# The first four m-tiles of a hybrid block on G*(x-s), corrected on their products, with the adaLN rounds in runs

## The chip, the cores and the metric

One core of one Trainium2 chip runs the whole program. The metric is the device time of one execution in microseconds. Before the change three runs took 2303.6 to 2304.38 us, median 2304.2 us.

## The reference, cut to what matters

Two post-LN layers, 512 latent tokens (l) and 256 context tokens (c), width 2048. Each layer modulates its normalised input by adaLN, projects it into the inputs of three mixers (latent attention, RG-LRU, retention), gates their outputs and projects back. What the change touches is the very beginning, for layer 0:

```python
mod = silu(cond) @ w_ada + b_ada          # shift, scale, gate; one set for l, one for c
h   = layer_norm(x) * (1 + scale) + shift # = G*(x-mu)*rstd + B
u   = h @ w_in                            # its columns: lru_x (512), lru_g, ret_..., mla_...
```

With s the value that is subtracted from x of a token first, layer_norm(x) is (x-s)*rstd - rmean, where rmean = (mu-s)*rstd. So h @ w is rstd*((G*(x-s)) @ w) - rmean*(G @ w) + B @ w.

## The kernel before, in words

Tensors lie transposed: 16 k-tiles of 128 features, each 128x512 (l) or 128x256 (c). Every fp32 product is done in three: the weight (`wh`, `wl`) and the token tile (`xh`, `xl`) are split in a high and a low part, and TensorE adds wh*xh, wh*xl and wl*xh into one PSUM tile. ScalarE copies the high parts, VectorE subtracts for the low ones. The order on each engine is the order in which the program calls it; nothing reorders. Background tasks (`spawn`) are generators; `step()`, called after every step of matmuls, resumes the first two of its list, or the first alone where a task is marked so. All loads are issued by SP, in one queue, by `fetch` (L168); every engine call is recorded at L158, every matmul at L204, transposes at L208.

The opening (L1515 to L1618) is written out by hand:

- SP loads all 16 k-tiles of x (256 KB) and c (128 KB), then the first 16 adaLN tiles, then three `wing` tiles (the weights of lru_x, 512 KB each, eight in all). Of the adaLN weights `wada` the opening reads 16 blocks of eight 128x512 tiles.
- The statistics: s is the mean of the first k-tile, VectorE subtracts it from x, ScalarE squares, TensorE adds both up with a 32-column matrix of ones; `fold2`, `finish` and `spread` make rstd and rmean, broadcast over the partitions.
- `Ada.steps` (L403) computes two blocks of adaLN: 16 `wada` tiles, 64 matmuls of 256 columns, in which four positions of 32 columns of the array each take one matmul of a set. Each set of four ends with a `yield`. Then ScalarE copies the result out, TensorE transposes it and VectorE reduces it.
- `first_norm` normalises two k-tiles in place (VectorE multiplies, POOL subtracts); `first` makes G and B for two k-tiles (`gb_block`), then h and its split: a VectorE multiply-add per tile (`x_high`), a high copy on ScalarE, a low part on VectorE. Into `res` go the tiles that are kept for later.
- `group(xps, j2, ...)` (L1582) multiplies k-tiles 2*j2 and 2*j2+1 into all four lru_x m-tiles: eight steps, of one k-tile and one m-tile each, six matmuls a step. The sums of all 16 k-tiles stay in PSUM: two `pa` tiles (two m-tiles of l each) and two `pb` tiles (of c). After each step `pause()` does the next set of the adaLN block that group j2+2 needs. So groups 0 to 5 have sets of adaLN between their steps and groups 6 and 7 have none.
- After group 7 `lru_pad` copies the four products into padded tiles, by turns on ScalarE and VectorE. It frees the `pa` tiles, of which there are two; the next projection (lru_g, in layer 0's loop from L1624) takes the first. The LRU tasks (convolution, gates, recurrence) are spawned then, behind `softplus_neg`.

`W` is the stream of projection weights: three buffers of 512 KB (`ws`), five high and four low parts; `W.get` hands out one k-tile and prepares the next four or five. Pools: `L` 48 tiles of 128x512, `C` 50 of 128x256, `aw` 3 of 128x512, `big` 2 of 128x1552, `pa` 2, `pb` 4.

Of the kernel before, what the change touches and what calls it, by code (L numbers as in the profile page):

```python
# [17 lines left out]
P = 128  # L18
# [18 lines left out]
AHEAD = 12  # L37
KEEP = {"l": 10, "c": 0}
# [47 lines left out]
def hybrid_kernel(ctx: ExitStack, tc: tile.TileContext, a, out_l):  # L86
# [140 lines left out]
    class Weights:  # L227
# [3 lines left out]
        def __init__(self, srcs, packed):  # L231
            self.srcs, self.packed, self.n, self.st, self.hl = srcs, packed, 0, {}, {}
# [35 lines left out]
        def prepare(self, i):  # L268
            for k in range(5):
                self.high(i + k)  # L270
                if k < 4:
                    self.low(i + k)

        def get(self):
            i = self.n
            self.n += 1
            self.prepare(i)
            self.load((i + 5) // 2)
            self.load((i + 7) // 2)
            return self.hl.pop(i)[:2]  # L280
# [109 lines left out]
    class Ada:  # L390
        def __init__(self, order):
            self.todo = [(cbs, n, q) for cbs in order for n in range(len(cbs)) for q in range(8)]
            self.w, self.n, self.nl = {}, 0, 0

        def load(self, i, slot):
            while self.nl < min(i, len(self.todo)):
                cbs, n, q = self.todo[self.nl]
# [5 lines left out]
        def steps(self, slot, ahead):  # L403

            cbs = self.todo[self.n][0]
            ps = PB()
            for n in range(len(cbs)):
                for q in range(0, 8, 2):
                    self.load(self.n + ahead, slot)
# [83 lines left out]

    def gb_block(l, j, n):

        for i in range(2):
# [5 lines left out]
            if l == 0:  # L502
                V.tensor_copy(B, sh)
            else:
                tt(B, G, pv(l - 1, "ln_b", j, n), op=OP.mult)
                tt(B, B, sh, op=OP.add)
                tt(G, G, pv(l - 1, "ln_g", j, n), op=OP.mult)
# [52 lines left out]
    def fold2(src, T):  # L560

        n = T // P
        ps = PB()
        for t in range(n):
            transpose(ps[:, t * P:(t + 1) * P], src[:, t * P:(t + 1) * P])
        v = ps[:, :T].rearrange("p (t g k r) -> p k t g r", g=2, k=2, r=32)
        o = SM(n, "fold"), SM(n, "fold")
        for k in range(2):
            V.tensor_reduce(o[k], v[:, k], axis=AX.XY, op=OP.add)
        return o  # L570

# [7 lines left out]
    class Stat:  # L579
        def __init__(self, T, parts, later=None):  # L580
            self.T = T
            self.s, self.sd, self.qd, self.sq = (v[:, 0:T] for v in parts)
            self.r, self.m = (v[:, 0:T] for v in later) if later else (self.s, self.sq)
# [23 lines left out]
        def finish(self, eps, rows=1):  # L607
            n = self.T // P
            if rows > 1:
                s, q = fold2(self.sd, self.T)  # L610
            else:
                yield self.sd, self.qd
                s = fold(self.sd, self.T)
                q = fold(self.qd, self.T)
            mu, v, t = SM(n, "st_mu"), SM(n, "st_v"), SM(n, "st_t")
            ts(mu, s, 1.0 / (D * rows), None, op0=OP.mult)
            tt(t, mu, mu, op=OP.mult)
            ts(v, q, 1.0 / (D * rows), eps, op0=OP.mult, op1=OP.add)
# [137 lines left out]
    def lru_pad(pss, b, eng):  # L756
# [3 lines left out]
        for s in "lc":  # L760
            o = b[:, PAD[s] + 2:PAD[s] + 2 + NT[s]]
            if eng == "a":
                copyA(o, pss[s])
            else:
                V.tensor_copy(o, pss[s])
# [750 lines left out]
    AD = Ada([(8 + j, j) for j in range(8)])  # L1516

    z0 = {"l": [], "c": []}
    stats, acc = {}, {}
    for j in range(NK):  # L1520
        for s, src in (("l", a["xT"]), ("c", a["cT"])):
            z = ST(s)
            fetch(z, src[j])
            z0[s].append(z)
    AD.load(16, LT)
    W.load(0)
    W.load(1)
    W.load(2)
    for s in "lc":
        b = BIG()  # L1530
        stats[s] = Stat(NT[s], [LT() for _ in range(4)], (b[:, 0:512], b[:, 512:1024]))
        ps = PB()
        mm(ps[:, :NT[s]], ones, z0[s][0], start=True, stop=True)
        copyA(stats[s].s, ps[:, :NT[s]])
    for s in "lc":
        acc[s] = PB()
    for j in range(NK + 1):
        for i, s in enumerate("lc"):
            T, st = NT[s], stats[s]
            if j < NK:  # L1540
                z = z0[s][j]
                tt(z, z, st.s, op=OP.subtract)
                act((st.sq, st.qd)[j % 2], z, AF.Square)
                g = 64 * ((j + i) % 2)
                mm(acc[s][g:g + 32, :T], one32, z, start=(j < 2), stop=(j >= NK - 2), tile_position=(0, g),
                   skip_group_check=True)
            if j > 0:
                g = 64 * ((j - 1 + i) % 2) + 32
                mm(acc[s][g:g + 32, :T], one32, (st.sq, st.qd)[(j - 1) % 2], start=(j < 3), stop=(j >= NK - 1),
                   tile_position=(0, g), skip_group_check=True)  # L1550
    for s in "lc":
        copyA(stats[s].sd, acc[s][:, :NT[s]])
    fin = [stats[s].finish(LN_EPS, 32) for s in "lc"]
    for n in range(3):
        for g in fin:
            next(g)
        if n == 1:
            for _ in AD.steps(LT, 20):
                pass
    for g in fin:  # L1560
        for _ in g:
            pass

    pl_, pc_ = [PA(), PA()], [PB(), PB()]
    xps = [{"l": pl_[j // 2][:, (j % 2) * 512:(j % 2) * 512 + 512],
            "c": pc_[j // 2][:, (j % 2) * 256:(j % 2) * 256 + 256]} for j in range(4)]

    def first_norm(j2):
        for k in (2 * j2, 2 * j2 + 1):
# [246 lines left out]
```

## Time and profile before

| what | value |
|---|---|
| median of 3 runs | 2304.2 us |
| profiled execution | 2304.76 us |
| its span, first to last instruction | 2303.0 us |
| mean granted TensorE clock, share of full | 0.996 |
| TensorE busy | 2251.0 us, 98% |
| VectorE busy | 71% |
| ScalarE busy | 46% |
| POOL busy | 15% |
| moved by DMA | 333.42 MB, mean 145 GB/s |

The busy times are shares of the whole span, in which the opening is the first 167.5 us. A stretch view gives for a part of the span the busy time of each engine, the granted clock of TensorE (1.00 is 2.4 GHz, 0.50 is 1.2 GHz), the DMA share (1.0 is 16 busy engines) and GB/s. Matmul records overlap, since a matmul's end is modelled; distances are therefore read from start to start. A timeline row holds one instruction, or a few of the same form (xN), and in brackets the idle time of the engine before it with what ended it. One adaLN matmul leaves two records.

### The profile page before, as it was taken

How to read it: one execution, taken by the hardware profiler on the slowest of the kernel's cores; microseconds unless marked ns; L12 is line 12 of the kernel's file. 1: busy time of each engine (PE TensorE's matmuls, PEld its weight loads, DVE VectorE, ACT ScalarE, POOL GpSimd, SP SyncE). 2: the span in 40 equal slices, each digit the busy share in tenths (PEclk: the TensorE clock that was granted, in tenths of full speed). 3: DMA queues.
4: the chain of work that ended last, by engine and by line, in shares of the span. 5: the costliest groups of instructions: out<-in, count | busy, mean ns of one | idle time of the engine just before them, and what ended most of it. 6: DMA issues, size and time to landing. Idle time of an engine off the chain costs nothing.

```text
span 2303.0 us, 35341 instructions
## 1 busy us (share of the span) xinstructions
PE 2251.0 (98%) x13162; PEld 1904.3 (83%) x13162; DVE 1642.7 (71%) x3043; ACT 1068.2 (46%) x1948; POOL 339.2 (15%) x291
## 2 busy tenths in 40 slices
PE   7999999999999999999999999999999999999998
PEld 3568888888888888888888978888888888888897
DVE  6655767887887777776876887666855347875677
ACT  4226766333333345553221487776333335554345
POOL 1310122221321100000111100111322200000112
PEclk9999999999999999999999999999999999999998
DMA  9963343334343431228654553453422222125365
GB/s 344 337 233 119 129 135 115 132 130 148 130 157 124 163 112 63 72 79 285 201 162 149 187 195 110 140 168 123 139 78 69 91 92 74 58 81 198 125 185 162
DMA packets 152200, 333.42 MB, mean 145 GB/s; under 512 B 17068, under 2 KB 35804, under 8 KB 152028
## 3 DMA queue, kind: packets, MB, share of 16 engines
q1 hardware_dynamic: 152028, 331.17, 43.5%
q8 instruction: 103, 1.69, 0.3%
q14 instruction: 69, 0.57, 0.1%
HBM read 292.30 MB, written 38.80 MB: 144 GB/s over the span
## 4 chain that ended last, share of the span: by engine, by line
PE 88%; DVE 5%; DMA 2%; ACT 2%; issue 2%; POOL 1%; SPq 0%; DVEq 0%; ACTq 0%; POOLq 0%
PE pa L204 75%; PE pb L204 11%; PE pb L208 3%; DMA L<-wada 1%; DVE L L158 1%; DVE wl L158 1%; DVE soft L158 1%; POOL L L158 1%; DVE acc L158 1%; DMA L<-xT 1%; DVE C L158 1%; ACT L L158 1%; ACT big L158 1%; DVE big L158 0%; DMA ws<-wing 0%
## 5 line engine op out<-in xcount | busy, mean ns | idle before, releaser
L204 PE MATMUL pa<-L,wh 128*128 128x512 f32 (+1 forms) x3968 | 1197.4, 385 | 7.9 <-ACT big L158 3.5
L204 PEld LDWEIGHTS pa<-L,wh 128*128 128x128 f32 x3968 | 660.1, 188 | 138.2 <-issue 21.1
L204 PE MATMUL pa<-L,wl 128*128 128x512 f32 (+1 forms) x2000 | 767.9, 384 | 1.7 <-DVE wl L158 1.7
L158 DVE TENSOR_TENSOR wl<-ws,wh 128x512 fp32r<-128x512 f32 x532 | 416.5, 791 | 328.1 <-PE pa L204 221.1
L158 ACT ACTIVATE wh<-ws 128x512 fp32r<-128x512 f32 x536 | 327.6, 625 | 379.1 <-PE pa L204 310.5
L204 PEld LDWEIGHTS pa<-C,wh 128*128 128x128 f32 x2240 | 412.1, 188 | 88.4 <-DVE C L158 1.5
L204 PE MATMUL pa<-C,wh 128*128 128x256 f32 x2240 | 444.5, 281 | 0.8 <-DVE C L158 0.8
L204 PEld LDWEIGHTS pa<-L,wl 128*128 128x128 f32 x2000 | 376.6, 188 | 39.3 <-issue 3.3
L158 DVE SCALAR_TENSOR_TENSOR acc<-aw,cond,acc 128x512 f32<-128x512 f32 x420 | 337.5, 840 | 7.7 <-DMA aw<-wadb 7.0
L204 PE MATMUL pa<-C,wl 128*128 128x256 f32 x1136 | 320.2, 282 | 1.7 <-DVE wl L158 1.7
L204 PEld LDWEIGHTS pa<-C,wl 128*128 128x128 f32 x1136 | 213.9, 188 | 3.8 <-DVE wl L158 1.9
L158 ACT ACTIVATE L<-L 128x512 fp32r<-128x512 f32 (+2 forms) x182 | 113.6, 628 | 217.1 <-DVE L L158 192.4
L204 PE MATMUL pb<-L,L 128*128 128x256 f32 (+2 forms) x1392 | 208.9, 345 | 4.8 <-DMA L<-wada 1.6
L158 POOL TENSOR_TENSOR L<-L,L 128x512 fp32r<-128x512 f32 (+1 forms) x80 | 119.9, 1498 | 391.5 <-ACT L L158 235.5
L204 PEld LDWEIGHTS pb<-L,L 128*128 128x128 f32 (+1 forms) x1392 | 133.8, 160 | 40.1 <-DMA L<-wada 17.0
L158 ACT ACTIVATE L<-pb 128x512 fp32r<-128x512 f32 (+2 forms) x156 | 87.6, 596 | 94.7 <-PE pb L204 63.8
L158 DVE TENSOR_TENSOR L<-L,L 128x512 fp32r<-128x512 f32 (+2 forms) x176 | 123.1, 701 | 11.3 <-ACT L L158 9.4
L158 ACT ACTIVATE L<-pa 128x512 f32<-128x512 f32 (+1 forms) x110 | 65.1, 595 | 142.3 <-PE pa L204 141.3
L204 PE MATMUL pa<-L,L 128*128 128x512 f32 x320 | 115.6, 401 | 1.1 <-ACT big L158 1.1
L158 DVE TENSOR_TENSOR L<-pb,L 128x512 fp32r<-128x512 f32 (+1 forms) x160 | 105.3, 682 | 9.9 <-PE pb L208 4.2
L158 ACT ACT_TABLE_LOAD x77 | 98.8, 1283 | 12.0 <-PE pa L204 5.2
L158 ACT ACTIVATE big<-pa,soft 128x768 f32<-128x768 f32 (+1 forms) x80 | 65.4, 818 | 76.0 <-DVE soft L158 75.6
(194 smaller groups left out, 2163.3 us busy)
## 6 DMA issues: line engine op xcount, KB each, us to landing
ws<-win SPq DMA_DIRECT2D x136, 512.0 KB, 3.5
aw<-wadb SPq DMA_DIRECT2D x256, 256.0 KB, 2.7
ws<-wout SPq DMA_DIRECT2D x94, 512.0 KB, 3.7
L<-wada SPq DMA_DIRECT2D x128, 256.0 KB, 5.7
ws<-wmla SPq DMA_DIRECT2D x20, 512.0 KB, 3.5
ws<-wing SPq DMA_DIRECT2D x16, 512.0 KB, 3.9
res_l<-L SPq DMA_DIRECT2D x32, 256.0 KB, 3.5
L<-res_l SPq DMA_DIRECT2D x32, 256.0 KB, 3.6
```

The costliest lines, as they stand in the source:

```text
L158: return f(o, *a, **k)
L204: nc.tensor.matmul(o, w, r, **kw)
L208: nc.tensor.transpose(o, i, ident[0:k, 0:k])
```

## The change

- The adaLN blocks are done one at a time, 16 rounds of eight tiles, in the order 8 9 10 11 0 12 1 ... 7. Blocks 8 to 15 give G, blocks 0 to 7 give B. All 16 matmuls of a round stand in one run, without a yield; then come two empty yields, the copy, two more, the transposes. Result and transposes share a PSUM bank.
- Groups run on G*(x-s) (`scaled`: high part by ScalarE with G as scale, low part by VectorE), so they need G of their two k-tiles and neither statistics nor B.
- Token pairs are loaded between adaLN tiles (`AD.before`); subtracting, squaring and adding up (`center`, `add_up`) hang on rounds 1 to 4 (`AD.then`); `statistics` runs in pieces in the pauses of group 2.
- `whole` makes the true h for all later projections, in pauses of groups 3 to 7 and, for the last pair, between the pads: two VectorE operations per tile to normalise in place (POOL has none left), G and B by ScalarE, high by ScalarE, low by VectorE. `lru_pad` multiplies by rstd on VectorE.
- `fix_pads`, first in the background list and alone in it, reads `wing` a second time, multiplies it by a matrix with the columns G and B of l and c (16 matmuls 32x512, in four parts), transposes and adds the two corrections to the four pads. `softplus_neg` and the LRU tasks stand behind it.
- adaLN tiles go into `aw`, thirds of `big` and `L`; how many tiles a round loads ahead stands in RING, by group. Four c tiles are kept in `res` early, and stored in pauses.

```diff
-AHEAD = 12
-KEEP = {"l": 10, "c": 0}
+RING = (15, 15, 15, 15, 13, 10, 8, 8)
+KEEP = {"l": 10, "c": 4}
+WHOLE = {3: (0, 1), 4: (2,), 5: (3,), 6: (4,), 7: (5, 6)}
...
                     self.load(self.n + ahead, slot)
-                    yield 0
-            ev = LT()
+            yield 0
+            yield 0
+            ev = LT()[:, 0:256]
             copyA(ev, ps)
             yield 3
-            pt = PB()
+            yield 3
...
-    def lru_pad(pss, b, eng):
+    def lru_pad(pss, b, scale=None):
...
-            if eng == "a":
+            if scale:
+                tt(o, pss[s], scale[s], op=OP.mult)
+            else:
                 copyA(o, pss[s])
-            else:
-                V.tensor_copy(o, pss[s])
...
-    AD = Ada([(8 + j, j) for j in range(8)])
+    AD = Ada([(b,) for b in (8, 9, 10, 11, 0, 12, 1, 13, 2, 14, 3, 15, 4, 5, 6, 7)])
...
+    for j in range(1, 8):
+        AD.before[4 * j + 4] = lambda j=j: tokens(j)
+        AD.then[4 * j + 4] = lambda j=j: (center(j), add_up(j - 1))
+    AD.then[36] = lambda: add_up(7)
...
+    def scaled(j2):
+
+        g_block(2 * j2, 2)
+        ks = [(s, k) for k in (2 * j2, 2 * j2 + 1) for s in "lc"]
+        for s, k in ks:
+            xt[s, k] = pair(s)
+            act(xt[s, k][0], z0[s][k], AF.Identity, scale=GB[0][:, "lc".index(s), 0, k:k + 1])
+        for s, k in ks:
+            stt(xt[s, k][1], z0[s][k], GB[0][:, "lc".index(s), 0, k:k + 1], xt[s, k][0].bitcast(F32),
+                op0=OP.mult, op1=OP.subtract)
+
+    def whole(j2):
+
+        b_block(2 * j2, 2)
+        ks = [(s, k) for k in (2 * j2, 2 * j2 + 1) for s in "lc"]
+        for s, k in ks:
+            z = z0[s][k]
+            tt(z, z, rstd[s], op=OP.mult)
+            tt(z, z, rmean[s], op=OP.subtract)
+            yield
+        h = []
+        for s, k in ks:
+            i = "lc".index(s)
+            xm, (xh, xl) = ST(s), pair(s)
+            act(xm, z0[s][k], AF.Identity, scale=GB[0][:, i, 0, k:k + 1], bias=GB[0][:, i, 1, k:k + 1])
+            copyA(xh, xm)
+            h.append((xm, xh, xl))
+            yield
+        for (s, k), v in zip(ks, h):
+            x_low(s, k, *v)
...
+    for i in range(8):
+        W.depth = (2, 3)[i] if i < 2 else 5
+        st = [AD.steps(slot, RING[i]) for _ in range(1 if i == 7 else 2)]
+        if i == 0:
+            work = chain(st[0], calls(lambda: scaled(1)), st[1])
+        else:
+            work = chain(*st)
+        also = statistics() if i == 2 else iter(())
...
+        if 0 < i < 7:
+            scaled(i + 1)
+        vec = chain(*[whole(j) for j in WHOLE.get(i, ())])
...
+            for _ in range(1 + (i in (3, 7))):
+                next(vec, None)
+
+        group(xps, i, "lc", lambda s, k: xt[s, k], pause)
+        for _ in chain(work, also) if i == 7 else chain(work, also, vec):
             pass
...
+        for q in range(4):
+            yield [w[4 * q + g] for g in range(4)]
+            for g in range(4):
+                k = 4 * q + g
+                mm(ps[32 * g:32 * g + 32, :], cv[:, k, :], w.pop(k), start=q == 0, stop=q == 3, tile_position=(0, 32 * g))
+            if q < 3:
+                for g in range(4):
+                    load(4 * q + 4 + g)
...
+        for j in range(4):
+            for i, s in enumerate("lc"):
+                z = pads[j][:, PAD[s] + 2:PAD[s] + 2 + NT[s]]
+                stt(z, rmean[s], o[:, j, i:i + 1], z, op0=OP.mult, op1=OP.add)
+                act(z, z, AF.Identity, bias=o[:, j, 2 + i:3 + i])
+            yield pads[j]
+
+    pads0 = []
+    for j in range(4):
+        if j % 2 == 0:
+            b = BIG()
+        if j == 2:
+            for _ in chain(vec, whole(7)):
+                pass
+        pads0.append(b[:, 776 * (j % 2):776 * (j % 2) + 776])
+        lru_pad(xps[j], pads0[j], rstd)
...
+    spawn(fix_pads(pads0), True)
     spawn(softplus_neg(), True)
```

How this moves the instructions, at three places. First TensorE at the start of group 0 of the changed kernel; `L_97` holds the conditioning, `aw`, `big` and `L` the adaLN tiles, `wh_304` is the first lru_x weight, `one_95` the ones of the statistics:

```order
L205 MATMUL pb_312<-L_241,L_97 32x256 x2
L205 MATMUL pb_312<-aw_243,L_97 32x256 x2
L205 MATMUL pb_312<-L_245,L_97 32x256 x2
L205 MATMUL pb_312<-big_237,L_97 32x256 x2
L209 MATMUL pb_312<-ident,L_360 128x128 x2
L205 MATMUL pa_383<-L_367,wh_304 128x512
L205 MATMUL pa_383<-L_368,wh_304 128x512
L205 MATMUL pb_385<-C_370,wh_304 128x256
L205 MATMUL pb_385<-C_371,wh_304 128x256
L205 MATMUL pb_287<-L_225,one_95 32x512
L205 MATMUL pb_287<-L_288,one_95 32x512
```

The first lru_x products (`pa_383`, `pb_385`) stand right behind the first round and its transposes, and the statistics' sums behind them; before, all 16 k-tiles of the statistics and two double blocks of adaLN stood ahead of the first product.

Then TensorE between two steps, before, in group 0 (`pb_798` is the next adaLN block, `pb_745` the one that has just been transposed):

```order
L204 MATMUL pb_694<-L_576,L_97 32x256 x2
L204 MATMUL pb_694<-L_578,L_97 32x256 x2
L208 MATMUL pb_745<-ident,L_743 128x128 x4
L204 MATMUL pa_627<-L_671,wh_639 128x512
L204 MATMUL pa_627<-L_672,wh_639 128x512
L204 MATMUL pb_629<-C_676,wh_639 128x256
L204 MATMUL pb_629<-C_677,wh_639 128x256
L204 MATMUL pa_627<-L_671,wl_640 128x512
L204 MATMUL pb_629<-C_676,wl_640 128x256
L204 MATMUL pb_798<-L_584,L_97 32x256 x2
L204 MATMUL pb_798<-L_586,L_97 32x256 x2
L204 MATMUL pa_627<-L_671,wh_639 128x512
```

and now, in group 7, with the last round, `pb_1824`:

```order
L205 MATMUL pb_385<-C_1638,wh_1472 128x256
L205 MATMUL pb_385<-C_1639,wh_1472 128x256
L205 MATMUL pb_1824<-aw_1728,L_97 32x256 x2
L205 MATMUL pb_1824<-L_1730,L_97 32x256 x2
L205 MATMUL pb_1824<-big_1736,L_97 32x256 x2
L205 MATMUL pb_1824<-L_1738,L_97 32x256 x2
L205 MATMUL pb_1824<-L_1744,L_97 32x256 x2
L205 MATMUL pb_1824<-aw_1746,L_97 32x256 x2
L205 MATMUL pb_1824<-L_1752,L_97 32x256 x2
L205 MATMUL pb_1824<-big_1736,L_97 32x256 x2
L205 MATMUL pa_383<-L_1635,wl_1473 128x512
L205 MATMUL pb_385<-C_1638,wl_1473 128x256
```

A set of four matmuls (two rows) followed each step; now 16 matmuls stand in one run, inside a step, and the steps between two rounds have nothing between them.

Last, VectorE ahead of the first projection, before (`big` are the pads, `pa_627` and `pa_628` the lru_x products):

```order
L158 TENSOR_TENSOR L_1764<-L_1762,L_1763 128x512
L158 TENSOR_TENSOR C_1769<-C_1767,C_1768 128x256
L158 TENSOR_TENSOR L_1774<-L_1772,L_1773 128x512
L158 TENSOR_TENSOR C_1779<-C_1777,C_1778 128x256
L158 TENSOR_TENSOR wl_1703<-ws_1373,wh_1702 128x512
L158 TENSOR_TENSOR wl_1788<-ws_1543,wh_1787 128x512
L158 TENSOR_TENSOR wl_1816<-ws_1543,wh_1815 128x512
L158 TENSOR_TENSOR wl_1846<-ws_1705,wh_1845 128x512
L158 COPY big_1902<-pa_627 128x512
L158 COPY big_1902<-pb_629 128x256
L158 COPY big_1913<-pa_628 128x512
L158 COPY big_1913<-pb_630 128x256
```

and now (`L_988` and `C_1045` are rstd, `L_1019` and `C_1047` rmean, `ada_106` the adaLN result, `L_457` to `C_463` the k-tiles 12 and 13):

```order
L159 TENSOR_REDUCE ada_106<-pb_1824 128x4
L159 TENSOR_TENSOR ada_106<-ada_106,par 128x4
...
L159 COPY gb_108<-ada_106 128x2x2
L159 TENSOR_TENSOR L_457<-L_457,L_988 128x512
L159 TENSOR_TENSOR L_457<-L_457,L_1019 128x512
L159 TENSOR_TENSOR C_459<-C_459,C_1045 128x256
...
L159 TENSOR_TENSOR wl_1818<-ws_1600,wh_1817 128x512
L159 TENSOR_TENSOR L_1923<-L_1921,L_1922 128x512
...
L159 TENSOR_TENSOR L_1935<-L_1933,L_1934 128x512
...
L159 TENSOR_TENSOR big_1965<-pa_383,L_988 128x512
L159 TENSOR_TENSOR big_1965<-pb_385,C_1045 128x256
L159 TENSOR_TENSOR big_1965<-pa_383,L_988 128x512
```

Between the reduce of the last round and the multiplications that free `pa_383` now stand the normalisation and the low parts of further k-tiles.

## Rows read from the trace of the kernel before

**Rows 1.** busy time by engine, from the page: us (share of the span) and instructions:

```profile
PE 2251.0 (98%) x13162; PEld 1904.3 (83%) x13162; DVE 1642.7 (71%) x3043; ACT 1068.2 (46%) x1948; POOL 339.2 (15%) x291
```

**Rows 2.** TensorE's timeline at the opening's end (start, duration, instruction, [idle before]):

```profile
167.49 0.62 PE L204 MATMUL pa<-L,wh 128*128 128x512 f32 x2
```

**Rows 3.** stretches of the opening: busy us, granted clock, DMA share, GB/s:

```profile
core 0: us, PE busy (x) PEld busy (x) DVE busy (x) ACT busy (x) POOL busy (x), PEclk, DMA share, GB/s
0.00:10.00 10.00, 4.12 (x9) 1.72 (x11) 2.85 (x11) 3.69 (x7) 0.20 (x4) 1.00 0.74 227
10.00:80.00 70.00, 60.50 (x455) 28.82 (x451) 51.90 (x119) 26.78 (x59) 19.09 (x16) 0.98 1.03 371
90.00:100.00 10.00, 10.00 (x80) 5.98 (x82) 8.82 (x16) 2.81 (x6) 4.10 (x4) 1.00 0.97 353
54.90:150.63 95.73, 91.32 (x700) 54.47 (x698) 63.67 (x132) 19.91 (x41) 28.34 (x36) 0.98 0.87 307
119.00:134.94 15.94, 15.22 (x120) 9.19 (x120) 10.65 (x22) 3.41 (x7) 4.66 (x4) 1.00 0.91 304
150.63:167.49 16.86, 16.86 (x100) 14.75 (x99) 8.02 (x22) 5.03 (x10) 0.00 (x0) 1.00 0.49 159
```

**Rows 4.** TensorE's timeline up to the first lru_x matmul:

```profile
50.96 0.62 PE L204 MATMUL pb<-L,L 128*32 128x256 f32 x4 [0.57 <-DMA L<-wada]
54.49 0.66 PE L208 MATMUL pb<-ident,L 128*128 128x128 f32 x4 [2.90 <-ACT L L158]
54.90 0.71 PE L204 MATMUL pa<-L,wh 128*128 128x512 f32 x2
```

**Rows 5.** TensorE's timeline inside an interleaved group:

```profile
61.82 0.72 PE L204 MATMUL pa<-L,wh 128*128 128x512 f32 x2
...
63.07 0.64 PE L204 MATMUL pb<-L,L 128*32 128x256 f32 x8
63.64 0.72 PE L204 MATMUL pa<-L,wh 128*128 128x512 f32 x2
```

**Rows 6.** DMA view of 0:168 us:

```profile
DMA packets 28444, 51.00 MB, mean 304 GB/s; under 512 B 3279, under 2 KB 6989, under 8 KB 28431
```

**Rows 7.** a half microsecond of TensorE's adaLN run (columns as in rows 3):

```profile
28.50:29.00 0.50, 0.50 (x16) 0.31 (x10) 0.43 (x5) 0.04 (x1) 0.00 (x0) 1.00 0.87 328
```

**Rows 8.** TensorE's timeline between two groups:

```profile
134.53 0.66 PE L208 MATMUL pb<-ident,L 128*128 128x128 f32 x4 [0.72 <-ACT L L158]
134.94 0.71 PE L204 MATMUL pa<-L,wh 128*128 128x512 f32 x2
```

**Rows 9.** VectorE's timeline behind the last adaLN block:

```profile
153.43 0.68 DVE L158 TENSOR_TENSOR L<-L,L 128x512 fp32r<-128x512 f32 x1
154.03 0.42 DVE L158 TENSOR_TENSOR C<-C,C 128x256 fp32r<-128x256 f32 x1
154.36 0.68 DVE L158 TENSOR_TENSOR L<-L,L 128x512 fp32r<-128x512 f32 x1
```

**Rows 10.** stretches behind two idle gaps (columns as in rows 3):

```profile
55.50:56.00 0.50, 0.50 (x4) 0.50 (x3) 0.47 (x4) 0.00 (x0) 0.00 (x0) 0.66 1.06 381
...
58.00:59.00 1.00, 1.00 (x5) 0.83 (x4) 1.00 (x2) 0.00 (x0) 1.00 (x1) 0.50 1.00 373
...
1384.00:1385.00 1.00, 1.00 (x5) 0.90 (x4) 0.57 (x2) 1.00 (x3) 0.00 (x0) 0.50 0.79 281
```

**Rows 11.** TensorE's timeline in attention, behind the second gap:

```profile
1383.37 1.18 PE L204 MATMUL pa<-L,wh 128*128 128x512 f32 x2 [2.62 <-ACT L L158]
```

**Rows 12.** stretches of the projections of layer 0 (columns as in rows 3):

```profile
167.50:450.00 282.50, 282.50 (x1614) 245.39 (x1613) 199.00 (x336) 175.01 (x290) 57.75 (x43) 1.00 0.39 128
450.00:650.00 200.00, 196.94 (x1134) 169.04 (x1134) 166.50 (x311) 69.11 (x120) 41.87 (x27) 1.00 0.43 142
```

**Rows 13.** waits of SP's queue up to 168 us: total, times, longest:

```profile
SPq L168 <- DVE wl L158: 27.3, 7, 10.1
SPq L168 <- DMA L<-wada: 22.8, 65, 1.0
```

More of the change, by code (lines that the diff above doesn't have):

```diff
@@ L268, in prepare @@
         def prepare(self, i):
-            for k in range(5):
+            for k in range(self.depth):
                 self.high(i + k)
@@ new lines, in hybrid_kernel, with slot @@
+    for j in range(1, 8):
+        AD.before[4 * j + 4] = lambda j=j: tokens(j)
+        AD.then[4 * j + 4] = lambda j=j: (center(j), add_up(j - 1))
+    AD.then[36] = lambda: add_up(7)
+    spare, turn = [], iter(range(10 ** 9))
+    def slot():
+        n = next(turn) % 5
+        if n == 0:
+            return adp.tile([P, 512], F32, name=nm("aw"), tag="aw")
+        if n != 2:
+            return LT()
+        if not spare:
+            b = BIG()
+            spare.extend(b[:, 512 * i:512 * i + 512] for i in range(3))
+        return spare.pop(0)
@@ L1551, in hybrid_kernel @@
[L1551 to L1566, printed above, removed]
@@ L1610, in hybrid_kernel, with chain, calls, pause @@
-    group(xps, 7, "lc")
+    def chain(*gs):
+        for g in gs:
+            yield from g
+    def calls(*fs):
+        for f in fs:
+            f()
+            yield
+    center(0)
+    for n in range(2):
+        W.high(n)
+        W.low(n)
+    for _ in AD.steps(slot, 15):
+        pass
+    scaled(0)
+    xps = group_psum()
+    for i in range(8):
[6 more added lines that the diff above has]
+        also = statistics() if i == 2 else iter(())
+        out = kept[:]
+        del kept[:]
+        if 0 < i < 7:
+            scaled(i + 1)
+        vec = chain(*[whole(j) for j in WHOLE.get(i, ())])
+        def pause():
+            next(work, None)
+            next(also, None)
+            if out:
+                s, k = out.pop(0)
+                nc.sync.dma_start(res[s][k], z0[s][k])
+            for _ in range(1 + (i in (3, 7))):
+                next(vec, None)
+        group(xps, i, "lc", lambda s, k: xt[s, k], pause)
+        for _ in chain(work, also) if i == 7 else chain(work, also, vec):
+            pass
@@ new lines, in fix_pads, with load @@
+    def fix_pads(pads):
+        cols = LT()
+        cv = cols.rearrange("p (k c) -> p k c", c=32)
+        V.memset(cols, 0.0)
+        for n in range(2):
+            V.tensor_copy(cv[:, :, 2 * n:2 * n + 2], GB[0][:, :, n, :].rearrange("p i k -> p k i"))
+        w = {}
+        def load(k):
+            w[k] = LT()
+            fetch(w[k], a["wing"][0, k // 2, :, k % 2 * 512:k % 2 * 512 + 512])
+        for k in range(4):
+            load(k)
+        yield cols
+        yield from take(1)
+        ps = PB()
+        for q in range(4):
[6 more added lines that the diff above has]
+                    load(4 * q + 4 + g)
+        yield ps
+        ev = LT()
+        copyA(ev, ps)
+        yield ev
+        pt = PB()
+        for j in range(4):
+            transpose(pt[:, j * P:(j + 1) * P], ev[:, j * P:(j + 1) * P])
+        give(1)
+        yield pt
+        o = CT()[:, 0:16].rearrange("p (j r) -> p j r", j=4)
+        V.tensor_reduce(o, pt.rearrange("p (j g r) -> p j r g", j=4, g=4)[:, :, 0:4, :], axis=AX.X, op=OP.add)
+        ts(o[:, :, 0:2], o[:, :, 0:2], -1.0, None, op0=OP.mult)
+        yield o
+        for j in range(4):
+            for i, s in enumerate("lc"):
+                z = pads[j][:, PAD[s] + 2:PAD[s] + 2 + NT[s]]
+                stt(z, rmean[s], o[:, j, i:i + 1], z, op0=OP.mult, op1=OP.add)
+                act(z, z, AF.Identity, bias=o[:, j, 2 + i:3 + i])
+            yield pads[j]
@@ L1611, in hybrid_kernel @@
+    pads0 = []
+    for j in range(4):
+        if j % 2 == 0:
+            b = BIG()
+        if j == 2:
+            for _ in chain(vec, whole(7)):
+                pass
+        pads0.append(b[:, 776 * (j % 2):776 * (j % 2) + 776])
+        lru_pad(xps[j], pads0[j], rstd)
     for k in range(NK):
@@ L1626, in hybrid_kernel @@
         if l == 0:
-            for j2 in range(2):
-                b = BIG()
-                for jj in range(2):
-                    pads.append(b[:, 776 * jj:776 * jj + 776])
-                    lru_pad(xps[2 * j2 + jj], pads[-1], "av"[jj])
+            pads = pads0
         gates = []
```

187 lines of the change are left out of this document (104 added, 83 removed).

## Prediction

> **What bounds the kernel now.** I start with the busy times: TensorE works 2251.0 of 2303.0 us [rows 1], so outside a few places the kernel is as long as TensorE's list of work. Everything the change touches lies ahead of the first gate projection, which starts at 167.49 us right behind the last lru_x matmul [rows 2]. So the second view is that opening, cut into stretches [rows 3]. Up to 80 us the DMA share is 1.0 at 371 GB/s: the opening is bound there by reading x, c and the first half of the adaLN weights. TensorE's list shows the same: idle times end with "DMA L<-wada", and the first lru_x matmul starts only at 54.90 us, after statistics and the first adaLN blocks [rows 4]. From 54.9 to 150.6 us it is TensorE that paces: 91.32 of 95.73 us busy, transfers at 307 GB/s; the last groups, with no adaLN between their matmuls, leave it no gap (16.86 of 16.86 us) [rows 3]. TensorE's timeline inside a group shows why these stretches are long: a step of six matmuls takes 1.25 us (61.82 to 63.07) plus 0.57 us for the four adaLN matmuls put behind it [rows 5]; in the plain groups 16 such steps take 16.86 us, 1.054 us each.
>
> The DMA view of the opening gives 51.0 MB up to 168 us [rows 6], of it 33.6 MB in the 128 adaLN tiles of 256 KB that the code loads, so at 371 GB/s these bytes alone would need 137 us. That is the floor which the change can approach.
>
> **The sum, part by part.** The profiled execution took 2304.76 us (0.56 above the median of 2304.2); I sum against its span of 2303.0 plus 1.8 around it.
>
> *Start of the products.* Group 0 no longer waits for statistics, only for two token pairs and the eight tiles of one adaLN round: 3.1 MB. From the rates [rows 3], 2.27 MB pass in the first 10 us and 0.371 MB per us after, so they are through at 12.3 us. The wait for the 32nd wada tile tells what comes on top: 16.5 MB stand in SP's order up to it, through at 10 + (16.5 - 2.27)/0.371 = 48.3 us, and its matmuls began at 50.96 [rows 4], 2.7 us later. I take 3: 15 us. Round, copy, transposes, reduce and the scaled tokens add some 5 us: group 0 starts at about 20 us instead of 54.9.
>
> *DMA, the new bound.* Ahead of the last adaLN tile SP now issues 128 wada, 16 xT, 16 cT, 8 wing, 2 win, 8 res_l and 4 res_c: 47.7 MB. 10 + (47.7 - 2.27)/0.371 + 3 gives 135.5 us. At 353 GB/s (90:100 [rows 3]) it would be 142 us.
>
> *TensorE against that.* Up to the last round's end it has 57 steps at 1.054 (60 us), 15 rounds, 8 `add_up` calls and 16 pairs of transposes. One round is 32 records; in the unbroken run of sets at 28 us [rows 7] 16 records took 0.5 us, so 1.07 us, plus 0.19 for what 1.25 has over 1.054: 1.26 us, 19 us in all. The upper bound is the interleaved price, 4 x 0.57 + 0.19 = 2.47 us, 37 us in all. I take the low one, because rows 7 have the same run of sets. `add_up` is 8 records 512 wide and 8 of 256 per call: between 0.8 us, by the same streaming, and twice that with its four changes of position; 1.4 each, 11 us in all; transposes 0.41 each time (134.53 to 134.94 [rows 8]), 6 us. Sum 20 + 96 = 116 us, or 134 us at the upper price: both before 135.5. So TensorE waits about 1 us per round, and DMA ends last. Waits of this length leave the granted clock alone (0.72 us ahead of 134.53 [rows 8]; the stretch 119 to 134.94, which begins behind a gap of the same kind, has 1.00 [rows 3]).
>
> *End of group 7.* Behind the last round (1.3) stand 7.4 steps (7.8) and transposes (0.5): 145 us.
>
> *The new wait in front of the first projection.* That projection takes the PSUM tile of m-tiles 0 and 1, which VectorE frees with `lru_pad`. In VectorE's order stand ahead of it: the reduce of round 15 (possible at 135.5 + 1.3 + 3.5 steps + 0.5 = 141), two low parts, `whole(6)` (eight tensor-tensor operations, spacing 0.60 and 0.33), one wl, four low parts, then the pad's first three operations. With the spacing of such operations [rows 9] and 0.35 for the reduce this is 0.35 + 0.95 + 3.7 + 0.6 + 1.9 + 1.6 = 9.1 us, and some 0.5 for ScalarE's copies between. The projection starts at about 150.5 us; TensorE idles 5 us (2 to 6). Before, the pads were plain copies that hid: the projection's first matmul has no idle time before it [rows 2]. The gain is 167.5 - 150.5 = 17.0 us.
>
> *Clock.* After the one comparable gap here, 2.90 us ahead of 54.49 [rows 4], the granted clock fell from 1.00 to 0.50 (1.2 GHz) between 55.5 and 59 us [rows 10]: 3.5 us at half pace, a loss of 1.8 us. A gap of 2.62 us ahead of 1383.37 [rows 11] had the same behind it [rows 10]. I charge 1.8 us once. The Trainium skill ("TensorE: Matmul & The Clock Gate", Why this matters for your kernels) advises against idle gaps between bursts of matmuls, because they bring the clock down to half. By that rule the trace agrees after these two gaps and not after the 0.72 us one, and it speaks against a change that trades a stream for bursts with waits. What the same mechanism would make of the whole opening, by the rows alone, is a rival below.
>
> *`fix_pads`, new on TensorE.* 16 matmuls 32x512 (32 records of 512 columns, as much as 64 of 256 at 1.07 us per 32: 2.1 us), four switches (0.2 to 0.4 each), four transposes with copy: 3.8 to 6.5 us; I take 4.6 us, nearest the streaming row. They stand between projections, where TensorE is full (282.50 of 282.50 us up to 450 [rows 12]), so they count in full. Its 16 transfers of 256 KB and its 16 operations on VectorE and ScalarE are hidden: there DMA share is 0.39 and VectorE 70% busy. SP's queue holds projection weights behind them, prefetched several k ahead.
>
> *What moves on.* VectorE does the normalisation (32 more operations of 0.6 or 0.33 us, that POOL did before) inside the opening, where it had 10.65 of 15.94 us [rows 3]: hidden except in the wait above. POOL gets lighter: nothing.
>
> *Later.* The LRU recurrences, which run beside the projections, wait for `fix_pads` and begin some 30 us later relative to TensorE's stream. VectorE has 30% slack up to 450 us but only 17% from 450 to 650 (166.50 of 200), where TensorE already idles 3.1 us [rows 12]. I take 0, with -1 to +3 us.
>
> Sum: 2304.8 - 17.0 + 1.8 + 4.6 = **2294.2 us**, some 0.4% below the median; own range 2286 to 2300. The low end has no wait (145 us, gain 22.4, no clock loss, 3.8 us for the pads: 2286); the high end has the last tile at 142 us.
>
> The transfer rate deserves a second look. The Trainium skill ("DMA: Bandwidth & Descriptors", Specifications) gives about 358 GB/s per core from HBM; by it 47.7 MB would be there 4.5 us later and the sum would be 2298.7. The 371 GB/s measured over 70 us of this trace decides, so I keep it.
>
> **The rivals.**
>
> *Better (10%): no wait in front of the projection.* If VectorE gets ahead, the price of the wait and of the clock goes: 2286 to 2288. Against it: its order is fixed, with `whole(6)` ahead of the pads.
>
> *Bursts on TensorE pace the opening (12%).* The rounds cost 2.47 us, 134 us in all, and waits ahead of some of them bring half clock, 1.8 us each. With four such drops the last round ends near 141 instead of 135.5 and the sum is 2300; a transfer rate of 353 gives the same. For: the two gaps of 2.90 and 2.62 us did it [rows 4, 10, 11]. Against: the 0.72 us one did not, and a busier TensorE has no gaps. It decides once the waits ahead of most rounds are like those two.
>
> *Given back later (9%).* From 80 us on DMA stays at the 307 GB/s of the stretch 54.9:150.6 [rows 3], since slots come free only when a round of eight tiles has run. 28.2 MB are through by then, the other 19.5 take 63.5 us: last tile at 146.5, projection at 161, gain 6.4, and with 1.8 and 4.6 charged the time is 2304.8: no change. For: SP waited 27.3 us for wl operations and 22.8 us for earlier adaLN transfers [rows 13]. Against: that low rate was TensorE's pace then, not the queue's.
>
> *Slower (8%): the LRU tasks pile up.* `fix_pads` stands alone at the head of the background list. The recurrences start 30 us later in TensorE's order, and VectorE, 83% busy from 450 to 650, makes up 0.17 us per us. If only half is made up before the outputs are needed near 850 us, TensorE waits 15 us there: 2294 + 15 = 2309, and with waits of the projections as now [rows 12] about 2312. It decides once the delay left at 850 us is some 15 us. Against: between 167.5 and 650 us VectorE has 482.5 - 365.5 = 117 us to spare [rows 12], far more than the delay.
>
> *The change does not do what it says (in the same 9%).* Group 0 could start late because its first round waits for its tiles behind others; the issue order, eight wada tiles right behind the first tokens, speaks against it.
>
> **Chances and range.** The forecast has 61%. What measurement can tell from no change is 0.2%, 4.6 us: faster means under 2299.6, slower over 2308.8. Forecast and better case give 0.71, and half of the bursts 0.06: faster 0.77. Same: half of the bursts and what is given back, 0.15. Slower: 0.08. The range runs from 2286 (better case) to 2304 (most of the given back); outside lie the slower case and the ends of the others.
>
> **What would show it.** Right: first lru_x matmul near 20 us; DMA share about 1.0 up to 130 us; adaLN rounds of 1.1 to 1.4 us; last round at 136 +- 4; first projection at 150.5 with 5 us of idle before it, released by VectorE's pads; 0.5 clock for some 3.5 us behind; `fix_pads` 4 to 6 us; everything later shifted by 10 us, with no new waits between 200 and 850 us. Wrong: a share under 0.9 between 30 and 130 us, half clock through much of the opening, idle of TensorE near 850 us, or a first projection after 158 us.

## The result and the profile after

The changed kernel takes 2329.6 us (median of 4 runs) against 2303.9 us: ratio 1.0112, 95% interval 1.01 to 1.0124. It is slower by 25.7 us where 10 us of gain were forecast. The page's busy times answer to [rows 1]; the span is 2328.3 us:

```profile
PE 2246.4 (96%) x13196; PEld 1911.6 (82%) x13196; DVE 1660.0 (71%) x3066; ACT 1114.5 (48%) x2025; POOL 300.2 (13%) x259
```

TensorE is busy 4.6 us less, in a span 25.3 us longer: the time went into waits. The opening did get shorter. TensorE's timeline of the changed kernel, at the first lru_x matmul, the last round and the first projection (for [rows 2, 4]):

```profile
16.71 0.44 PE L209 MATMUL pb<-ident,L 128*128 128x128 f32 x2 [2.13 <-ACT L L159]
18.64 0.57 PE L205 MATMUL pa<-L,wh 128*128 128x512 f32 x1 [1.49 <-ACT L L159]
...
70.96 1.12 PE L209 MATMUL pb<-ident,L 128*128 128x128 f32 x4 [2.96 <-ACT L L159]
...
141.55 0.41 PE L205 MATMUL pb<-aw,L 128*32 128x256 f32 x2
...
143.42 0.50 PE L205 MATMUL pa<-L,wl 128*128 128x512 f32 x1
...
151.35 0.28 PE L205 MATMUL pb<-C,wl 128*128 128x256 f32 x1
157.39 1.22 PE L205 MATMUL pa<-L,wh 128*128 128x512 f32 x2 [5.76 <-DVE big L159]
```

The first projection starts at 157.39 us instead of 167.49. The stretches of the opening (for [rows 3]), and the clock behind the 5.76 us wait:

```profile
10.00:80.00 70.00, 61.86 (x495) 36.38 (x494) 32.91 (x83) 32.91 (x68) 0.00 (x0) 0.93 1.00 365
80.00:100.00 20.00, 19.34 (x170) 14.83 (x172) 14.54 (x35) 12.98 (x25) 0.00 (x0) 1.00 0.93 316
100.00:120.00 20.00, 16.93 (x151) 12.34 (x144) 18.05 (x42) 14.14 (x28) 0.00 (x0) 1.00 0.96 332
120.00:140.00 20.00, 20.00 (x178) 14.94 (x178) 14.31 (x36) 12.37 (x24) 0.27 (x6) 1.00 1.04 388
...
160.00:161.00 1.00, 1.00 (x5) 0.90 (x4) 0.96 (x2) 1.00 (x2) 0.00 (x0) 0.50 0.89 323
163.00:164.00 1.00, 1.00 (x8) 0.87 (x7) 0.75 (x2) 0.97 (x3) 0.00 (x0) 1.00 0.00 0
```

To see where the lead was lost, I counted the product matmuls into `pa` (`pa<-L,wh` and `pa<-L,wl`, 5968 in each kernel) in the traces of several kernels and took the start of the n-th, as us later (+) than in the kernel before:

| n-th | before at | after | e1_hold | e3_lane | e8_early_lane | e15_runs |
|---|---|---|---|---|---|---|
| 292 | 203.5 | -4.2 | -2.4 | -4.6 | -2.4 | -12.1 |
| 1700 | 767.8 | -2.4 | +7.3 | +6.8 | +1.1 | -12.1 |
| 2700 | 1241.8 | -1.0 | +11.0 | +11.8 | +4.2 | -12.4 |
| 2900 | 1354.3 | +25.8 | +29.5 | +11.9 | +4.7 | -12.5 |
| 5500 | 2224.9 | +26.4 | +30.7 | +9.5 | +3.3 | -12.5 |

(Background matmuls shift between the counted ones, so single cells are good to 1 or 2 us.) Up to 1242 us the changed kernel is still ahead. Then 26.8 us go in one place, between layer 0's last output projection and layer 1's first product. TensorE's timeline there, after:

```profile
1331.82 0.28 PE L205 MATMUL pa<-C,wl 128*128 128x256 f32 x1
1349.66 1.64 PE L205 MATMUL pb<-acc,one 128*32 128x256 f32 x8 [17.57 <-DVE acc L159]
1351.78 0.69 PE L209 MATMUL pb<-ident,acc 128*128 128x128 f32 x2 [0.48 <-ACT acc L159]
1356.86 0.80 PE L205 MATMUL pa<-L,wh 128*128 128x512 f32 x1 [4.39 <-ACT L L159]
```

and VectorE's:

```profile
1334.90 15.28 DVE L159 SCALAR_TENSOR_TENSOR acc<-aw,cond,acc 128x512 f32<-128x512 f32 x22
```

These 22 operations are the end of what layer 1 needs from `ada_rest`, the lane that computes the last four adaLN blocks of layer 0 and then those of layer 1 on VectorE. `norm_task` of layer 0 waits for G and B of layer 1, so 15.3 us of VectorE work, the sums, the transposes and the first normalisation stand in a row. In the kernel before TensorE has no wait for `acc` between 1250 and 1420 us: by 1320 us its lane had run 396 operations, the changed kernel's 362, which with these 22 makes 384. The clock falls as well:

```profile
1340.00:1345.00 5.00, 0.00 (x0) 0.00 (x0) 4.95 (x8) 0.00 (x0) 0.00 (x0) 0.50 0.71 191
...
1360.00:1365.00 5.00, 5.00 (x15) 3.92 (x14) 4.93 (x9) 4.90 (x9) 0.00 (x0) 0.62 0.72 244
```

Why is the lane late? The view of the tile `acc` up to 850 us gives its operations, 267 + 18 before and 228 + 16 after:

```profile
L158 DVE SCALAR_TENSOR_TENSOR acc<-aw,cond,acc x267: 734/744/1789, 197.7 to 825.8; 128x512 f32<-128x512 f32 x134
L158 DVE TENSOR_SCALAR acc<-aw,cond x18: 475/478/482, 185.1 to 785.6; 128x512 f32<-128x512 f32 x18
```

```profile
L159 DVE SCALAR_TENSOR_TENSOR acc<-aw,cond,acc x228: 733/745/1794, 178.3 to 823.5; 128x512 f32<-128x512 f32 x114
L159 DVE TENSOR_SCALAR acc<-aw,cond x16: 472/479/1515, 177.5 to 799.3; 128x512 f32<-128x512 f32 x16
```

41 operations are missing, about 30 us of VectorE at 0.74 each. (The expectations below count 301 and 238 from merged timeline rows; these are the exact numbers, 285 and 244.) The lane does not lose them at once: by 450 us it had run 74 operations before and 71 now. What falls behind up to 450 us is VectorE's work as a whole, 178.57 us of it against 199.00 [rows 12], and from 450 to 650 us it is busier than before, 173.07 us against 166.50 [rows 12]:

```profile
167.50:450.00 282.50, 282.50 (x1628) 242.37 (x1628) 178.57 (x313) 172.67 (x287) 41.48 (x33) 1.00 0.41 133
450.00:650.00 200.00, 196.82 (x1120) 169.51 (x1119) 173.07 (x298) 72.44 (x123) 54.40 (x36) 1.00 0.40 132
```

Ahead of that stands `fix_pads`. Its four quarters run 7 us apart, since each waits for four loads, and everything in the background list waits behind it:

```profile
176.74 1.06 PE L205 MATMUL pb<-L,L 128*32 128x512 f32 x8
184.21 1.07 PE L205 MATMUL pb<-L,L 128*32 128x512 f32 x8
191.41 1.07 PE L205 MATMUL pb<-L,L 128*32 128x512 f32 x8
198.24 1.06 PE L205 MATMUL pb<-L,L 128*32 128x512 f32 x8
201.10 0.60 PE L209 MATMUL pb<-ident,L 128*128 128x128 f32 x4
```

The first scan of an LRU, on VectorE, in the kernel before and in the changed one:

```profile
230.35 0.69 DVE L158 TENSOR_TENSOR_SCAN C<-C,C 128x256 f32<-128x256 f32 x1
```

```profile
275.09 0.69 DVE L159 TENSOR_TENSOR_SCAN C<-C,C 128x256 f32<-128x256 f32 x1
```

44.7 us later, although TensorE was 4 us ahead by then. The order on VectorE is decided when the program is written out: by the scheduler's own clock, `step()` resumes a background task while the engines are less than 1.9 us ahead (SLACK[0]), the lane only below 0.3 us (SLACK[1]), or -0.3 us (SLACK[2]) while a task that must run alone, as `fix_pads` and the LRU tasks must, is in the list. Background work that comes later therefore displaces the lane.

### The profile page after: what moved, and what is told of

Same layout as the page of the kernel before. It is cut to its first block, busy times and chain, and to the rows that moved or that the text cites. A ratio compares the mean times of both kernels' runs of the same rounds, so it can differ in the third digit from the quotient of the medians.

```text
span 2328.3 us, 35434 instructions
## 1 busy us (share of the span) xinstructions
PE 2246.4 (96%) x13196; PEld 1911.6 (82%) x13196; DVE 1660.0 (71%) x3066; ACT 1114.5 (48%) x2025; POOL 300.2 (13%) x259
## 5 line engine op out<-in xcount | busy, mean ns | idle before, releaser
L159 DVE TENSOR_TENSOR wl<-ws,wh 128x512 fp32r<-128x512 f32 x532 | 411.0, 780 | 348.3 <-PE pa L205 221.7
L159 DVE SCALAR_TENSOR_TENSOR acc<-aw,cond,acc 128x512 f32<-128x512 f32 x420 | 346.9, 863 | 4.4 <-DMA aw<-wadb 3.6
L205 PE MATMUL pb<-L,L 128*128 128x256 f32 (+3 forms) x1216 | 199.1, 344 | 3.4 <-POOL L L159 2.7
L159 DVE TENSOR_TENSOR L<-L,L 128x512 f32<-128x512 f32 (+2 forms) x208 | 147.6, 711 | 15.1 <-ACT L L159 11.5
L159 ACT ACTIVATE L<-pb 128x512 fp32r<-128x512 f32 (+3 forms) x166 | 90.5, 576 | 70.8 <-PE pb L205 36.3
```

What stands on the lines that cost most here:

```text
L159: return f(o, *a, **k)
L205: nc.tensor.matmul(o, w, r, **kw)
```

## Experiments

Theory T: the late start of the background list costs the time, through VectorE. Rival R: the work that the change adds costs it.

**e1_hold**: the kernel before, plus a delay that does no work.

```diff
+    def hold():
+        end = clk[0] + 60.0
+        while clk[0] < end:
+            yield 0.3
+
+    spawn(hold(), True)
     spawn(softplus_neg(), True)
```

> The kernel before, with one task put alone at the head of the background list, ahead of softplus_neg and the LRU tasks; it does no work and ends after 60 us of the scheduler's own clock. Theory T (the change is slow because the LRU tasks start late, the background list stays long, and the adaLN lane of VectorE for layer 1 gets too few steps before attention): this kernel too has fewer than 260 acc steps before 850 us (before: 301), TensorE waits 10 to 20 us for acc behind the last output projection of layer 0, and the time is 2316 to 2326 us. Rival R (the work that the change adds to VectorE and TensorE makes it slow, not the late start): no work is added here, so 2304 +- 4 us and no such wait.

Measured: 2334.5 us, 1.0133 (1.0117 to 1.0148). The delay alone costs more than the whole change. Operations on `acc` up to 850 us: 256; first scan at 289.73. TensorE's waits between 1250 and 1420 us (total, times, longest):

```profile
PE pb L204 <- DVE acc L158: 9.2, 1, 9.2
PE pa L204 <- ACT L L158: 7.0, 2, 4.4
```

R is excluded as the main cause. VectorE's work from 167.5 to 450 us falls here too, to 180.96 us against 199.00 [rows 12]. The time is 8.5 us over my range. The wait is 9.2 us, a little under what I expected, but 11 us were lost before it (the table): lateness shows up in two places.

**e10_hold25**: the same with `+ 25.0`.

> The kernel before with the idle head task of e1_hold shortened from 60 to 25 us of the scheduler's clock. T2: the price grows with the delay; the lane's plan gives it 265 steps at attention against 256 in e1_hold and 286 in the kernel before, so most of e1_hold's price is already there: 2314 to 2326 us, with a wait for acc behind the last output projection of 3 to 9 us. R2 (a delay is absorbed until VectorE's spare time is used up): 2304 to 2309 us.

Measured: 2313.4 us, 1.0038 (1.0025 to 1.0051), with a 5.0 us wait for acc, 265 operations up to 850. Price and lane grow with the delay; my lower end was 0.6 us too high.

**e2_no_fix**: the changed kernel without `spawn(fix_pads(pads0), True)`.

> The changed kernel without fix_pads: the two corrections of the pads are left out, with their loads, matmuls and VectorE work; everything else stays. T: the LRU tasks start some 40 us earlier, the lane is only a little behind, the 17.6 us wait for acc shrinks to under 4 us, and with the 4.9 us of the matmuls the time falls to 2298 to 2305 us. R: only the work of fix_pads itself goes, 5 us on TensorE: 2323 to 2326 us, and the wait for acc stays over 12 us.

Measured: 2296.9 us, 0.997 (0.9959 to 0.9982); no wait for acc, 271 operations, first scan at 230.93, and VectorE's work from 167.5 to 450 us is back at 202.72 us. That is 32.7 us less than the changed kernel, of which TensorE's own part of `fix_pads` is 5 us. The lateness alone would be some 22 us, by my estimate: first scans 21.6 and 59.4 us late (e10_hold25, e1_hold) cost 8.5 and 30.9 us, and a straight line between them gives that for the changed kernel's 44.7. The 5 or 6 us left over were not traced; the VectorE work and the loads of `fix_pads`, which this run also leaves out, are not excluded for them.

**e3_lane**: the lane gets its steps back.

```diff
-SLACK = [1.9, 0.3, -0.3, -0.5, 2.5]
+SLACK = [1.9, 0.6, 0.0, -0.5, 2.5]
```

> The changed kernel with two numbers of the scheduler raised, SLACK[1] from 0.3 to 0.6 and SLACK[2] from -0.3 to 0.0, so that the adaLN lane is resumed sooner beside the background tasks; no work is added or left out. T: acc steps before 850 us are back near 300, the 17.6 us wait and the half clock behind it go, 2302 to 2308 us. R (VectorE is physically full between 450 and 850 us): the background tasks come late instead and TensorE waits as long for them before 850 us: 2320 us or more.

Measured: 2314.4 us, 1.0045 (1.0029 to 1.0062). Between the two. The wait for acc at layer 1 is gone (270 + 18 operations up to 850), but the table shows 9.2 us lost against the changed kernel by 768 us. TensorE's waits in 450:850 us went from 2.9 us before, all for POOL, and 5.1 us in the changed kernel, to 9.2 us:

```profile
PE pb L205 <- POOL L L159: 3.0, 5, 1.3
PE pb L209 <- DVE rsq_r L159: 2.1, 1, 2.1
PE pb L205 <- POOL C L159: 2.1, 3, 1.3
PE pb L205 <- DVE acc L159: 1.2, 2, 1.1
PE pb L205 <- ACT C L159: 0.5, 1, 0.5
PE pb L205 <- ACT L L159: 0.3, 1, 0.3
```

and the granted clock was 0.91 to 0.97 in three 20 us stretches. So T becomes T2: VectorE time is lost at the start (the 20 us up to 450 us above) and is missing later; the scheduler only chooses who is late.

**e14_before_lane**: the same two numbers in the kernel before, as a control.

> The kernel before with SLACK[1] and SLACK[2] raised to 0.6 and 0.0, as in e3_lane and e8_early_lane: what the two numbers do alone. In the kernel before the lane is not late, so T2 expects nothing to gain: 2302 to 2307 us. Rival (the numbers are better for any order, and e3_lane and e8_early_lane gained from that): under 2300 us.

Measured: 2307.2 us, 1.001 (1.0001 to 1.0019), 0.2 us over the upper end. They are no improvement by themselves.

**e7_early16** (all 16 loads of `fix_pads` ahead of the stores to `res`), **e8_early_lane** (eight of them, with e3's numbers), **e9_early16_lane** (all 16, SLACK[1] = 0.6 alone). The edit, with 8 or 16:

```diff
-        for k in range(4):
+        for k in range(8):
             load(k)
+        yield
         yield cols
...
+    fix = fix_pads(pads0)
+    next(fix)
     for k in range(NK):
...
-    spawn(fix_pads(pads0), True)
+    spawn(fix, True)
```

> The changed kernel with all 16 loads of fix_pads issued at once, ahead of the stores to res, instead of four at a time behind them; nothing else. Its four quarters should run back to back and the first LRU scan should start near 240 us instead of 275. Theory T2 (the VectorE time that is lost between 157 and 213 us, while the background list stands behind fix_pads, is missing later, and the scheduler only chooses who is late; it still leaves the adaLN lane last): the acc steps before 850 us stay within 10 of the 238 of the changed kernel, the LRU and retention work is earlier, the wait for acc stays over 10 us: 2318 to 2326 us. Rival R2 (only the late LRU start counts): the wait goes as in e2_no_fix, 2298 to 2306 us.

Measured: 2327.2 us, 1.0101 (1.0084 to 1.0118): 249 operations, 11.9 us of wait for acc; the first scan came at 257.77, not 240. T2's picture, 1 us outside its numbers.

> The changed kernel with the first 8 loads of fix_pads ahead of the stores and two quarters in flight, and SLACK[1] and SLACK[2] raised to 0.6 and 0.0 as in e3_lane. T2: the lane is on time as in e3_lane (2314 us) and the background tasks some 15 us earlier, so TensorE's extra waits before 850 us fall from about 9 to 3 us: 2304 to 2309 us. R2': start and lane are independent, and the loss before attention stays: 2312 to 2316 us.

Measured: 2307.0 us, 1.0013 (1.0003 to 1.0022): as T2 said, with both remedies the loss against the kernel before is all but gone; TensorE's waits in 450:850 us are 4.5 us.

> The changed kernel with all 16 loads of fix_pads at once, ahead of the stores, and SLACK[1] raised to 0.6 alone: the lane gets its steps back only after the LRU tasks are done. T2: no wait for acc, and the LRU start earliest of all versions that do the whole work: 2297 to 2304 us, faster than both kernels if anything is. Rival (VectorE is full in any order): 2308 us or more.

Measured: 2312.6 us, 1.0035 (1.0022 to 1.0048): a miss, with the rival's number. There is no wait for acc, as T2 said; against the rival, VectorE was far from full at the start. 16 loads in one block hold up SP's queue: TensorE waits 2.3 us for `wing`, the lane's own loads come behind, and VectorE is busy 13.4 us of the 40 from 160 to 200, where the changed kernel had 21.4.

**e4_pads**: `whole(6)` moved behind the first two pads.

```diff
-WHOLE = {3: (0, 1), 4: (2,), 5: (3,), 6: (4,), 7: (5, 6)}
+WHOLE = {3: (0, 1), 4: (2,), 5: (3,), 6: (4,), 7: (5,)}
...
-            for _ in chain(vec, whole(7)):
+            for _ in chain(vec, whole(6), whole(7)):
```

> The changed kernel with whole(6) moved from group 7 to behind the first two pads, beside whole(7), so that VectorE frees the first lru_x PSUM tile earlier. T: TensorE's 5.8 us wait in front of the first projection falls under 1.5 us and the half clock behind it (some 2.4 us) goes; the first projection starts at about 151 us instead of 157.4; all that follows keeps its order, so the time is 2320 to 2323 us. Rival (the lane's end bounds the time, whatever the opening does): 2328 to 2330 us, with a longer wait for acc at the end of layer 0.

Measured: 2336.5 us, 1.0136 (1.0121 to 1.0151): a miss, of both ranges. The projection did start 6.3 us earlier, at 151.11, but most of the wait came back, with half clock behind it (0.50 from 168 to 170 us), and the wait for acc was still 16.7 us. TensorE's timeline:

```profile
166.89 0.51 PE L205 MATMUL pa<-L,wl 128*128 128x512 f32 x1 [2.35 <-DVE wl L159]
176.41 2.95 PE L205 MATMUL pb<-L,L 128*32 128x512 f32 x8 [1.39 <-DMA L<-wing]
```

The `wl` part stands behind `whole(7)` and the pads on VectorE, and the `wing` tiles are not there earlier. By the 400th product (242.7 us before) its lead is 6.1 us, 1.4 more than the changed kernel's. Why its median lies 7 us above the changed kernel's is open; its profiled execution, with a span of 2329.8, is its fastest run.

**e13_e8pads** and **e12_pool2**: the same move in e8_early_lane; in e12 also `whole(7)` behind all four pads, and the subtraction of rmean in `whole(6)` and `whole(7)` on POOL.

> e8_early_lane with whole(6) behind the first two pads as in e4_pads, all on VectorE. From e4_pads, where a start 7 us earlier was gone 50 us later (waits for wl and for wing): no gain, 2304 to 2309 us. Rival (the wait ahead of the first projection was real loss): 2298 to 2302 us.

> e8_early_lane, with whole(6) behind the first two pads and whole(7) behind all four, and the subtraction of rmean in both on POOL, which is idle there. VectorE then frees the first lru_x tile some 7 us earlier and has 16 operations fewer between 150 and 166 us than in e4_pads, where the saved wait came back as waits for wl and wing. T2: no wait of 5.8 us, no half clock behind it, under 2 us of waits for wl: 8 us better than e8_early_lane at 200 us, and 2297 to 2302 us, faster than both kernels. Rival (as in e4_pads, the VectorE work between the pads is only waited for elsewhere): 2304 to 2308 us.

Measured: 2308.8 us, 1.0018 (1.0009 to 1.0027), as expected; and 2309.7 us, 1.0025 (1.0016 to 1.0034), outside both ranges and nearer the rival's. In e12 the saved 5.8 us came back as 5.2 us for `wl` and 4.4 us for `wing`:

```profile
169.18 0.75 PE L205 MATMUL pa<-L,wl 128*128 128x512 f32 x1 [5.22 <-DVE wl L159]
182.77 4.25 PE L205 MATMUL pb<-L,L 128*32 128x512 f32 x8 [4.37 <-DMA L<-wing]
```

**e15_runs**: one part of the change alone, in the kernel before: adaLN in runs (with 16 tiles loaded ahead), no `fix_pads`, LRU tasks where they were.

```diff
-AHEAD = 12
+AHEAD = 16
...
+                for _ in range(3):
+                    yield 0
                 for q in range(0, 8, 2):
...
                     self.load(self.n + ahead, slot)
-                    yield 0
+                yield 0
```

> One part of the change alone, in the kernel before: the adaLN matmuls between the steps of groups 0 to 5 stand in runs of 16 (eight tiles) behind every fourth step, where four stood behind every step, and 16 tiles are loaded ahead instead of 12. Statistics, normalisation, pads and the whole background list stay as before, without fix_pads, so the LRU tasks and the adaLN lane keep their places in the order. T2 (the change lost by starting the LRU tasks late, and its opening as such is a gain): groups 0 to 5 take about 13 us each instead of 16, paced by the transfers, the first projection starts near 155 us instead of 167.5, nothing is given back later: 2291 to 2296 us, faster than both kernels. Rival (16 slots free only in runs, so transfers stay at 307 GB/s): 2301 to 2305 us.

Measured: 2293.2 us, 0.9954 (0.9941 to 0.9968), 10 us faster than the kernel before. Its groups, and a run with the step behind it:

```profile
54.90:140.00 85.10, 80.62 (x698) 58.13 (x698) 63.70 (x136) 19.94 (x41) 28.36 (x36) 1.00 0.94 342
```

```profile
71.68 1.93 PE L204 MATMUL pb<-L,L 128*32 128x256 f32 x32
73.54 0.72 PE L204 MATMUL pa<-L,wh 128*128 128x512 f32 x2
...
155.34 0.63 PE L204 MATMUL pa<-L,wh 128*128 128x512 f32 x2
```

Four sets in a run take 1.86 us, start to start, and some 0.2 more on the two steps beside them, where four apart took 4 x (0.57 + 0.19) = 3.0 us with what they add to their steps [rows 5]. Groups 0 to 5 have 12 such runs (a double block is 32 matmuls, not 64; they leave 64 records), so some 1 us each makes the lead of 12 us. DMA moves 342 GB/s instead of 307, and the first projection starts at 155.34. The table shows that the lead is kept to the end: 286 operations on `acc` by 850 us, one more than before.

## Why the prediction was wrong

Step by step, in the prediction's order:

- *Start of the products*: forecast 20 us, measured 18.64. Right.
- *DMA and TensorE in the opening*: the last round was forecast at 135.5 and came at 141.55. The floor by the transfers was about right (365 GB/s up to 80 us), but behind group 0's start TensorE waited for an adaLN tile only once, 0.5 us at 37.7, and from 120 to 140 us it was busy all 20.00 us: TensorE paced the end. Its sum was too small: the 96 us charged from group 0's start to the end of the last round took 124.8 (18.64 to 143.42). Read from start to start, the 15 rounds took 32.8 us where 19 were charged, the products 66.6 for 60, part of it at half clock, `add_up` 13.3 for 11, the transposes 4.1 for 6; and TensorE waited 8.0 us that I had left out, 6.7 of them for the copies ahead of transposes. A round by itself takes 1.87 us (141.55 to 143.42), not 1.26: a half-microsecond stretch also counts the records of 0.39 us that only reach into it, so the 16 of [rows 7] were no rate (16 x 0.5/(0.5 + 0.39) = 9 in half a microsecond make 1.8 us per round). The rival of bursts had this in part: the 15 rounds took 2.2 us each, nearer its 2.47, and the last one came at its 141 us. Of its four drops of the clock there were two, one behind the waits ahead of 16.71 and 18.64, one behind that ahead of 70.96.
- *The wait in front of the first projection*: forecast 5 us, released by the pads; measured 5.76, released by `big`. The chain on VectorE was right. Its half clock lasted until about 162.3 us, some 5 us, and cost 2.4 us where 1.8 were charged. The Trainium skill ("TensorE: Matmul & The Clock Gate", Why this matters for your kernels) advises against long idle gaps between bursts of matmuls, because they bring the clock down to half. The trace agrees here, and again behind the 17.57 us at 1332 us; the 0.72 us gap that the prediction holds against the advice is no long one. The projection started 10.1 us earlier than before, not 17.0, so with half clock and `fix_pads` some 3 us of gain were left (4.2 in the table at 203.5 us), not 10.6.
- *`fix_pads`*: forecast 4.6 us on TensorE, measured 4 x 1.07 + 0.6 = 4.9. Right. What I wrote of the rest, that its work and loads are hidden, was the error.
- *Later: "I take 0"*: this is the step that failed. I saw that the LRU tasks would begin some 30 us later (45 in fact), and set against it 117 us of spare VectorE time [rows 12]. But spare time is only of use where there is work ready for it. While the list stood behind `fix_pads` there was too little: VectorE did 20 us less work up to 450 us than before. From 450 to 650 us it was 87% busy, and the lane goes last. The background tasks did catch up, so little showed up to 850 us, where I looked: TensorE waited 5.1 us from 450 to 850 us, 2.2 more than before. The adaLN lane did not, and its deadline is at 1332 us.
- *The slower rival* had the right cause (8%), but the wrong victim, place and price: TensorE idle near 850 us for 15 us, 2309 to 2312. The runs showed 26.8 us at 1332 us.

The opening as such was a gain: e2_no_fix shows it without the correction and its price. Most of it, if not all, is the runs: e15_runs, with the old statistics and first product, has its first projection at 155.34, 2 us ahead of the changed kernel. No run has the earlier first product (18.64 us instead of 54.90) without the runs, and nothing here shows that it adds to their gain. The three effects add up: 4.2 us ahead at 203.5 us, 3.2 us lost by 1242 us, 26.8 us at the end of layer 0, 25.8 us behind.

Not tried: doing the products of `fix_pads` inside the opening while the `wing` tiles are in SBUF, so that the pads are ready with the last group.

## What to carry to other kernels

When a change delays a task that others queue behind, follow every queue to its own deadline, the one with the lowest priority first: the price is paid where that work is due, here some 1100 us after the change. A sum of spare engine time over hundreds of microseconds is no cover; it must lie where the delayed work is ready. A delay that does no work, put into the kernel before, shows such a price in one run, and one part of the change alone can keep the gain.

## What the runs showed of the hardware that was not expected

Half clock outlasted each long gap: behind 2.90 us of idle it ended 4 to 5 us after TensorE's return [rows 4, 10], behind 2.96 us (ahead of 70.96) about 6 us after it, behind 5.76 us about 5 us after it, and behind the 17.57 and 4.39 us waits it held from before 1340 to about 1364 us. Idle of 1.17 and 1.91 us in the opening, at 111 and 105 us, left it at 1.00 (100:120 above). Adjacent adaLN sets on TensorE cost 0.47 us each in a run (1.86 for four, with some 0.2 on the steps beside it), and 0.57 with 0.19 more on the step when they stand alone [rows 5]: most of a set's time is not the change between the two kinds of matmul.
